# A gated SiLU over 201 MB: loads and stores change queues, most activations and multiplies take 4 rows instead of 2

## Chip, cores, metric

One core of a Trainium2 chip runs the whole program, which uses no other core. The metric is device time in microseconds (us). Before the change: median 471.02 us of 3 runs (470.53 to 471.09).

## The reference

```python
x = randn(32, 512, 2048)              # float32
x1, x2 = x[..., :1024], x[..., 1024:]
out = (x1 * (1 / (1 + exp(-x1)))) * x2   # silu(x1) * x2, float32
```

That is 134.22 MB to read and 67.11 MB to write, with one activation and one multiply per output element.

## The kernel before

The 16,384 rows are cut into 16 tiles of 128 partitions x 8 rows. A tile is one load of 8.39 MB and one store of 4.19 MB; each partition's share is one contiguous piece of 64 KB (load) or 32 KB (store). Two input and two output buffers. ScalarE (ACT) computes silu, VectorE (DVE) multiplies, 2 rows at a time. ScalarE also issues the loads, SyncE (SP) the stores. The first load is placed ahead of the barrier at the program's start.

```python
K, KC = 8, 2
in_pool  = tile_pool(bufs=2);  out_pool = tile_pool(bufs=2)

def load(i):
    xt = in_pool.tile([P, K, in_cols], dt, name="xt")
    nc.scalar.dma_start(out=xt[...], in_=view(x_flat, i))

load(0); load(1)
for i in range(n_tiles):
    ot = out_pool.tile([P, K, half], dt, name="ot")
    for c in range(0, k, KC):
        nc.scalar.activation(out=ot[:, c:ce, :], in_=xt[:, c:ce, :half], func=Silu)
        nc.vector.tensor_mul(out=ot[:, c:ce, :], in0=ot[:, c:ce, :], in1=xt[:, c:ce, half:])
        if last:
            nc.sync.dma_start(out=ov[:, c:ce, :], in_=ot[:, c:ce, :])   # last tile: 4 stores
    if not last:
        nc.sync.dma_start(out=ov, in_=ot[:, :k, :])
    if i + 2 < n_tiles:
        load(i + 2)
# (cut: views, pools' set-up, launch)
```

Of the kernel before, what the change touches and what calls it, by code (L numbers as in the profile page):

```python
# [1 line left out]

# [4 lines left out]


def issue_ahead_of_the_first_barrier(nc):




    head, body = nc.main_func.blocks[:2]
    load = next(ins for ins in body.instructions if type(ins).__name__ == "InstDMACopy")
    at = next(
        j for j, ins in enumerate(head.instructions)
        if ins.engine == load.engine and type(ins).__name__ == "InstDrain"
    )
    body.instructions = [ins for ins in body.instructions if ins.name != load.name]  # L20
    head.instructions = head.instructions[:at] + [load] + head.instructions[at:]


@with_exitstack
def kernel(
    ctx: ExitStack,
    tc: tile.TileContext,
    x: bass.AP,
    out: bass.AP,
):  # L30






    nc = tc.nc
    P = nc.NUM_PARTITIONS

    x_flat = x.flatten_outer_dims()  # L40
    out_flat = out.flatten_outer_dims()
    num_rows, in_cols = x_flat.shape
    half = in_cols // 2
    dt = x_flat.dtype

    K = 8
    KC = 2
    PLAN = [K] * (num_rows // (P * K))

    in_pool = ctx.enter_context(tc.tile_pool(name="in_pool", bufs=2))  # L50
    out_pool = ctx.enter_context(tc.tile_pool(name="out_pool", bufs=2))

    plan = []
    row = 0
    for k in PLAN:
        plan.append((row, k))
        row += P * k
    assert row == num_rows
    n_tiles = len(plan)

    def view(flat, i):
        row0, k = plan[i]
        return flat[row0:row0 + P * k].rearrange("(p k) d -> p k d", k=k)

    nc.at_finalize(issue_ahead_of_the_first_barrier)


    ctx.enter_context(tc.manual_schedule())

    loaded = {}  # L70

    def load(i):
        xt = in_pool.tile([P, K, in_cols], dt, name="xt")
        nc.scalar.dma_start(out=xt[:, :plan[i][1], :], in_=view(x_flat, i))
        loaded[i] = xt

    load(0)
    load(1)
    for i in range(n_tiles):
        k = plan[i][1]  # L80
        xt = loaded.pop(i)
        last = i == n_tiles - 1
        ov = view(out_flat, i)
        ot = out_pool.tile([P, K, half], dt, name="ot")
        for c in range(0, k, KC):
            ce = min(c + KC, k)
            nc.scalar.activation(  # L87
                out=ot[:, c:ce, :],
                in_=xt[:, c:ce, :half],
                func=mybir.ActivationFunctionType.Silu,  # L90
            )
            nc.vector.tensor_mul(  # L92
                out=ot[:, c:ce, :],
                in0=ot[:, c:ce, :],
                in1=xt[:, c:ce, half:],
            )
            if last:
                nc.sync.dma_start(out=ov[:, c:ce, :], in_=ot[:, c:ce, :])
        if not last:
            nc.sync.dma_start(out=ov, in_=ot[:, :k, :])  # L100
        if i + 2 < n_tiles:
            load(i + 2)


# [1 line left out]
_INS = ['x']  # L106
_OUTS = [((32, 512, 1024), 'float32')]


# [23 lines left out]
```

## Time and profile before

| What | Value | Where it is read |
|---|---|---|
| Time | 471.02 us | median of 3 runs |
| Span of the profiled execution | 468.9 us | page, first line |
| VectorE, ScalarE busy | 30%, 25% | page, part 1 |
| DMA engines busy | 99.6% (66.4 + 33.2) | page, part 3 |
| Rate in the middle of the run | 434 GB/s | table of windows |
| First store issued | 32.74 us | timeline |

The page of the kernel before, parts 1 to 3: busy time of the compute engines, busy share of the 16 DMA engines in 40 equal slices (in tenths), and the two DMA queues.

```profile
span 468.9 us, 269 instructions
DVE 142.3 (30%) x64; ACT 118.2 (25%) x65; POOL 0.2 (0%) x4
...
DMA  9899999999999998999999999999999989999998
...
q10 hardware_dynamic: 2304, 134.22, 66.4%
q1 hardware_dynamic: 2736, 67.11, 33.2%
```

The DMA row reads 9 in all slices but four, which read 8 (a digit is the share in tenths, and 9 means 90% or more); no compute engine comes near that. Queue 10 is ScalarE's (loads), queue 1 SyncE's (stores).

The table of windows of the kernel before; the last two columns are the DMA engines' share and GB/s.

```profile
core 0: us, DVE busy (x) ACT busy (x) POOL busy (x), PEclk, DMA share, GB/s
22.00:45.00 23.00, 8.90 (x4) 7.64 (x5) 0.00 (x0) 1.00 0.95 393
45.00:74.00 29.00, 8.89 (x4) 7.32 (x5) 0.00 (x0) 1.00 1.00 434
161.00:277.00 116.00, 35.58 (x16) 29.17 (x17) 0.00 (x0) 1.00 1.00 434
277.00:393.00 116.00, 35.58 (x16) 28.89 (x16) 0.00 (x0) 1.00 1.00 434
```

Every 29 us tile moves 12.58 MB at 434 GB/s. The Trainium skill ("DMA: Bandwidth & Descriptors", section "Where 436 GB/s comes from") works out 435.2 GB/s as the ceiling of the 16 ports; this trace agrees within 0.3%. Only the two ends are below it: the first 45 us, and the last 18 us (375 GB/s from 451 us on).

The timeline of the kernel before: start, duration, engine, instruction.

```profile
21.88 7.31 ACT L87 ACTIVATE ot<-xt 128x2048 f32<-128x2048 f32 x4 [19.31 <-DMA xt<-in_x_dram]
23.82 8.90 DVE L92 TENSOR_TENSOR ot<-ot,xt 128x2048 f32<-128x2048 f32 x4 [23.82 <-ACT ot L87]
...
32.74 23.00 SPq L100 DMA_DIRECT2D out_dram<-ot  x2
32.75 0.35 ACTq L74 DMA_DIRECT2D xt<-in_x_dram  x1
44.54 7.31 ACT L87 ACTIVATE ot<-xt 128x2048 f32<-128x2048 f32 x4 [15.36 <-DMA xt<-in_x_dram]
...
451.03 7.31 ACT L87 ACTIVATE ot<-xt 128x2048 f32<-128x2048 f32 x4 [21.57 <-DMA xt<-in_x_dram]
```

A tile is computed in 10.85 us (21.88 to 32.73); then the store and the load of the tile after next are issued. Load 0 is in SBUF at 21.88, the last one at 451.03 us.

The chain of waits of the kernel before, by engine:

```profile
DMA 80%; DVE 15%; ACT 3%; DVEq 0%; issue 0%
```

The 15% and 3% are not time that faster compute would win: while the chain sits there, the DMA engines move the other load and a store at full rate.

### The profile page before, as it was taken

The numbers are of one execution on the slowest core, as the hardware profiler recorded it, in microseconds if no ns is written. First come the engines' busy times: TensorE is split into PE (matmuls) and PEld (weight loads), VectorE is DVE, ScalarE is ACT, GpSimd is POOL, SyncE is SP. The second block draws the span as 40 slices with busy tenths as digits, with TensorE's granted clock in tenths as the row PEclk, the third lists the DMA queues.
The fourth block names the chain that finished last, engine by engine and source line by source line (L and its number), as shares of the span: only waits on it lengthen the run. The fifth ranks groups of instructions, "written<-read, shape, count | busy, mean of one in ns | idle before, by whom it ended". The sixth has DMA issues, their size and how long they took to land.

```text
span 468.9 us, 269 instructions
## 1 busy us (share of the span) xinstructions
DVE 142.3 (30%) x64; ACT 118.2 (25%) x65; POOL 0.2 (0%) x4
## 2 busy tenths in 40 slices
DVE  0070705106061160601507025070250702407034
ACT  1142406023060330603206032060420604106051
POOL 0000000000000000000000000000000000000000
DMA  9899999999999998999999999999999989999998
GB/s 431 375 447 403 447 447 447 403 419 431 447 447 403 447 492 363 442 492 391 458 403 439 456 447 403 409 442 447 447 403 444 467 386 447 442 419 481 400 409 354
DMA packets 5042, 201.35 MB, mean 429 GB/s; under 512 B 560, under 2 KB 560, under 8 KB 560
## 3 DMA queue, kind: packets, MB, share of 16 engines
q10 hardware_dynamic: 2304, 134.22, 66.4%
q1 hardware_dynamic: 2736, 67.11, 33.2%
q14 instruction: 2, 0.02, 0.0%
HBM read 134.22 MB, written 67.11 MB: 429 GB/s over the span
## 4 chain that ended last, share of the span: by engine, by line
DMA 80%; DVE 15%; ACT 3%; DVEq 0%; issue 0%
DMA xt<-in_x_dram 80%; DVE ot L92 15%; ACT ot L87 3%; DVEq L128 0%
## 5 line engine op out<-in xcount | busy, mean ns | idle before, releaser
L92 DVE TENSOR_TENSOR ot<-ot,xt 128x2048 f32<-128x2048 f32 x64 | 142.3, 2286 | 319.5 <-ACT ot L87 319.5
L87 ACT ACTIVATE ot<-xt 128x2048 f32<-128x2048 f32 x64 | 116.9, 1897 | 338.8 <-DMA xt<-in_x_dram 338.8
L87 ACT ACT_TABLE_LOAD x1 | 1.3, 1283 | 1.3 <-PEq L117 1.3
L117 POOL MEMSET const-uint8-127<- 128x1 uint8 x1 | 0.1, 102 | 0.0
L117 POOL MEMSET const-bfloat16-1.0<- 128x1 bf16 x1 | 0.1, 101 | 0.0
L117 POOL MEMSET const-float32-0.0<- 128x1 f32 x1 | 0.1, 98 | 0.2 <-issue 0.2
L117 POOL MEMSET const-float32-1.0<- 128x1 f32 x1 | 0.1, 98 | 0.0
## 6 DMA issues: line engine op xcount, KB each, us to landing
out_dram<-ot SPq DMA_DIRECT2D x15, 4096.0 KB, 39.8
out_dram<-ot SPq DMA_DIRECT2D x4, 1024.0 KB, 5.7
xt<-in_x_dram ACTq DMA_DIRECT2D x16, 47.1
```

Source lines behind the costliest of these rows:

```text
L87: nc.scalar.activation(out=ot[:, c:ce, :], in_=xt[:, c:ce, :half], func=mybir.ActivationFunctionType.Silu,)
L92: nc.vector.tensor_mul(out=ot[:, c:ce, :], in0=ot[:, c:ce, :], in1=xt[:, c:ce, half:],)
L117: nc = _bacc.Bacc("TRN2", target_bir_lowering=False, num_devices=1)
```

## The change

Its intent: take all waiting for buffers off ScalarE's queue, by giving SyncE the loads (the first still ahead of the barrier) and ScalarE the stores in program order; and pay fewer fixed costs with 4 rows per instruction in all tiles but the last. In the last tile each of the four stores is issued two steps late, so that ScalarE does not wait for VectorE between activations.

```diff
-    KC = 2
+    KC = 4
+    KC_LAST = 2
...
-        nc.scalar.dma_start(out=xt[:, :plan[i][1], :], in_=view(x_flat, i))
+        nc.sync.dma_start(out=xt[:, :plan[i][1], :], in_=view(x_flat, i))
...
+        if i < n_tiles - 1:
+            for c in range(0, K, KC):
+                silu(ot, xt, c, c + KC)
+                mul(ot, xt, c, c + KC)
+            nc.scalar.dma_start(out=ov, in_=ot)
+            if i + 2 < n_tiles:
+                load(i + 2)
+            continue
+
+        cuts = list(range(0, K, KC_LAST))
+        for n, c in enumerate(cuts + [None, None]):
+            if c is not None:
+                silu(ot, xt, c, c + KC_LAST)
+                mul(ot, xt, c, c + KC_LAST)
+            if n >= 2:
+                b = cuts[n - 2]
+                nc.scalar.dma_start(out=ov[:, b:b + KC_LAST, :], in_=ot[:, b:b + KC_LAST, :])
```

(`silu` and `mul` are the two calls of the kernel before, put into functions.)

More of the change, by code (lines that the diff above doesn't have):

```diff
@@ L73, in load, with silu, mul @@
         xt = in_pool.tile([P, K, in_cols], dt, name="xt")
-        nc.scalar.dma_start(out=xt[:, :plan[i][1], :], in_=view(x_flat, i))
+        nc.sync.dma_start(out=xt[:, :plan[i][1], :], in_=view(x_flat, i))
         loaded[i] = xt
+    def silu(ot, xt, c, ce):
+        nc.scalar.activation(
+            out=ot[:, c:ce, :],
+            in_=xt[:, c:ce, :half],
+            func=mybir.ActivationFunctionType.Silu,
+        )
+    def mul(ot, xt, c, ce):
+        nc.vector.tensor_mul(
+            out=ot[:, c:ce, :],
+            in0=ot[:, c:ce, :],
+            in1=xt[:, c:ce, half:],
+        )
     load(0)
@@ L79 @@
     for i in range(n_tiles):
-        k = plan[i][1]
         xt = loaded.pop(i)
-        last = i == n_tiles - 1
         ov = view(out_flat, i)
         ot = out_pool.tile([P, K, half], dt, name="ot")
-        for c in range(0, k, KC):
-            ce = min(c + KC, k)
-            nc.scalar.activation(
-                out=ot[:, c:ce, :],
-                in_=xt[:, c:ce, :half],
-                func=mybir.ActivationFunctionType.Silu,
-            )
-            nc.vector.tensor_mul(
-                out=ot[:, c:ce, :],
-                in0=ot[:, c:ce, :],
-                in1=xt[:, c:ce, half:],
-            )
-            if last:
-                nc.sync.dma_start(out=ov[:, c:ce, :], in_=ot[:, c:ce, :])
-        if not last:
-            nc.sync.dma_start(out=ov, in_=ot[:, :k, :])
-        if i + 2 < n_tiles:
-            load(i + 2)
+        if i < n_tiles - 1:
[14 more added lines that the diff above has]
+                nc.scalar.dma_start(out=ov[:, b:b + KC_LAST, :], in_=ot[:, b:b + KC_LAST, :])
 _INS = ['x']
```

## The prediction

> **What bounds the kernel now.** The DMA engines. The page's slices show them 98-99% busy throughout; VectorE 30%, ScalarE 25%. The table of windows gives 434 GB/s in every steady stretch (44 to 160 us). Successive tiles' activations start 29.0 us apart (timeline); a tile is 8.39 MB read + 4.19 MB written: 434 GB/s. The Trainium skill ("DMA: Bandwidth & Descriptors", "Where 436 GB/s comes from") puts the ceiling of the 16 ports at 435.2 GB/s; the trace agrees within 0.3%. The trace's packet records: a 64 KB load packet takes 2.418 us, a 32 KB store packet 1.213, an 8 KB one 0.309. One engine's share is 128, 120 and 32 of these, an estimated 465.0 us of work; packets run from 1.14 to 467.62 us of the 468.9 us span. So only about 1.5 us of that window is idle. The chain of waits (DMA 80%, DVE 15%, ACT 3%) misleads: while it sits on VectorE, the DMA engines move the other load and a store.
>
> **What the change moves.**
> - Queues swapped: loads to SP, stores to ACT. Same bytes, same transfers. The same page ("Issuing engines are not separate DMA queues") says both feed the same 16 engines; I expect the same packet times. SP's first instruction is 0.13 us ahead of ACT's first issue (trace), so the first load may start about 0.1 us earlier.
> - Activations and multiplies of 4 rows: 1.893 and 2.284 us for 2 rows now; fixed part estimated at 0.15-0.2 us, so 3.6 and 4.4 us for 4. About 5 us saved on each engine, off the critical path, worth nothing. From load landed to store and next load issued: 10.85 us now (timeline), about 12.5 after.
> - Are those 1.6 us hidden? Yes: when a store is issued, the previous one still has about 8 us of packets to go (packet records), and the load in flight about 18 us. Neither queue runs dry. An activation's wait for the store two tiles earlier has about 6 us of slack.
> - ScalarE waits for each tile's last multiply before issuing its store; it idles 22 us per tile for the load anyway.
> - The last tile keeps 2 rows, but its first store now follows the third activation: 5.7 us instead of 4.26 after landing. Its packets are wanted when tile 14's store ends, 8 us after the last load's packets; loads should end about 0.5 us earlier. At most a few tenths of DMA idle. The fourth store is issued at 10.9 us as before, 2.6 us before its turn.
>
> **Critical path.** Practically none of it: -0.1 us at the start, 0 in the middle, 0 to +0.5 us at the end. At most 1.5 us of idle could be won.
>
> **Prediction.** 471.0 us, 8 in 10 between 469.6 and 472.4. Faster by over 2%: 1%; within 2%: 97%; slower by over 2%: 2%.
>
> **What would show it right.** Steady windows at 434 GB/s, tile period 29.0 us; activation about 3.6 us x30, multiply about 4.4 us x30; load landed to next load issue about 12.5 us; the last load landing 0 to 1 us before 451.0; first packet near 1.0 us; span 468.5 to 469.5; the four last stores still back to back.
>
> **What would make it wrong.** Different arbitration or packet times when loads sit on the other queue; a DMA hole (share well under 1.00) in each tile, because the store queue runs dry and loads alone do not reach 434 GB/s; a hole above 1 us before the last tile's first store; the first load not starting early on SP.

## The result

471.81 us, median of 4 runs (471.35, 471.60, 472.01, 472.40), against 471.00 of the kernel before (4 runs by then): ratio 1.002, 95% interval 1.0002 to 1.0037. A ratio is the mean time of one kernel's runs over that of the other's of the same rounds, so it is not quite the ratio of the medians. It is 0.8 us more, and the four runs spread over 1.05 us where the kernel before's spread over 0.56.

The page of the changed kernel, parts 1 to 3:

```profile
span 469.8 us, 207 instructions
DVE 140.3 (30%) x34; ACT 115.4 (25%) x35; POOL 0.2 (0%) x4
...
DMA  9999989999999999999999999999999999999997
...
q1 hardware_dynamic: 2304, 134.22, 66.3%
q10 hardware_dynamic: 2736, 67.11, 33.1%
```

The queues have swapped, bytes and packets are the same, compute is 2 to 3 us less busy, the DMA row is as full. The span is 0.9 us longer.

Its groups of instructions (line, engine, operation, shapes, count, then busy us and mean ns of one):

```profile
L86 DVE TENSOR_TENSOR ot<-ot,xt 128x4096 f32<-128x4096 f32 x30 | 131.4, 4422 | 303.9 <-ACT ot L79 303.9
L79 ACT ACTIVATE ot<-xt 128x4096 f32<-128x4096 f32 x30 | 106.8, 3608 | 321.1 <-DMA xt<-in_x_dram 321.1
```

Its table of windows:

```profile
22.00:45.00 23.00, 8.76 (x2) 6.97 (x2) 0.00 (x0) 1.00 0.99 407
45.00:74.00 29.00, 8.76 (x2) 7.12 (x2) 0.00 (x0) 1.00 1.00 434
161.00:277.00 116.00, 35.04 (x8) 28.49 (x8) 0.00 (x0) 1.00 1.00 434
277.00:393.00 116.00, 35.04 (x8) 28.49 (x8) 0.00 (x0) 1.00 1.00 434
```

The middle is untouched: 434 GB/s, share 1.00. So nothing is lost per tile. Its timeline:

```profile
21.85 7.12 ACT L79 ACTIVATE ot<-xt 128x4096 f32<-128x4096 f32 x2 [19.79 <-DMA xt<-in_x_dram]
25.50 8.76 DVE L86 TENSOR_TENSOR ot<-ot,xt 128x4096 f32<-128x4096 f32 x2 [25.50 <-ACT ot L79]
34.29 0.38 ACTq L102 DMA_DIRECT2D out_dram<-ot  x1
45.85 7.12 ACT L79 ACTIVATE ot<-xt 128x4096 f32<-128x4096 f32 x2 [16.88 <-DMA xt<-in_x_dram]
...
451.92 5.51 ACT L79 ACTIVATE ot<-xt 128x2048 f32<-128x2048 f32 x3 [21.89 <-DMA xt<-in_x_dram]
```

Load 0 lands as before (21.85 against 21.88 us), but load 1 lands at 45.85 instead of 44.54, and the last load at 451.92 instead of 451.03. The loss happens once, between 22 and 46 us, where the first store is issued (34.29 instead of 32.74 us).

The GB/s column does not explain it, because it is a mean over 16 engines, and counts a packet whole in the stretch in which it starts. The packet records do. They carry no engine number, but an engine works through its packets one after another, so that each packet can be chained to the one that ended a few ns before it; that gives 16 chains. L is a 64 KB load packet, S a 32 KB store packet, with start and, in brackets, duration, in us of the span. A steady L lasts 2.42, a steady S 1.21. A load's share on an engine ends with a completion packet of 4 bytes (0.009 us, left out here), which takes a turn of its own between two S. Two typical engines of the kernel before, then a typical one of the changed kernel and its odd one:

```
before, engine a   L33.26(2.44) L35.70(3.18) S38.88(1.21) L40.09(2.42) S42.50(1.21)
before, engine b   L33.45(2.44) L35.89(3.38) S39.26(1.21) L40.47(2.42) S42.89(1.21)
after,  typical    L33.11(2.44) L35.54(2.42) L37.95(3.50) S41.45(1.21) S42.66(1.21) L43.87(2.42)
after,  odd one    L33.49(2.42) L35.90(3.05) S38.94(1.21) L40.15(4.11) S44.26(1.21) S45.47(1.21)
```

Each engine stalls once: the load packet just ahead of its first store takes 0.8 to 1.0 us too long before, 1.0 to 1.6 after. In the changed kernel one engine takes its first store a packet earlier than the other 15, and it pays twice: 0.63 us in the packet before its first store, and 1.69 us in the packet that it works on while the others stall. It ends its share of load 1, completion packet included, at 45.5 us, 2.3 to 2.9 us after the others (42.6 to 43.2). A load has landed only when its slowest engine is done, so load 1 lands late; and the engine stays behind for the rest of the run, because every engine has a fixed share of the transfers (128 L, 120 S and 32 packets of 8 KB each) and none idles to catch up in. Its last packet ends at 468.55 us. The other engines' last packets end between 467.05 and 467.72. In the kernel before all 16 end between 466.8 and 467.63.

The engines are never idle meanwhile: between 22 and 46 us the count of packets in flight never falls below 16 in either kernel.

### The profile page after: what moved, and what is told of

It reads as the page before. It is cut to its first block, busy times and chain, and to the rows that moved or that the text cites. A ratio compares the mean times of both kernels' runs of the same rounds, so it can differ in the third digit from the quotient of the medians.

```text
span 469.8 us, 207 instructions
## 1 busy us (share of the span) xinstructions
DVE 140.3 (30%) x34; ACT 115.4 (25%) x35; POOL 0.2 (0%) x4
## 4 chain that ended last, share of the span: by engine, by line
DMA 77%; DVE 14%; ACT 6%; DVEq 0%; issue 0%; ACTq 0%
DMA xt<-in_x_dram 77%; DVE ot L86 14%; ACT ot L79 6%; DVEq L140 0%; ACTq L79 0%
## 5 line engine op out<-in xcount | busy, mean ns | idle before, releaser
L86 DVE TENSOR_TENSOR ot<-ot,xt 128x4096 f32<-128x4096 f32 (+1 forms) x34 | 140.3, 4170 | 322.5 <-ACT ot L79 322.5
L79 ACT ACTIVATE ot<-xt 128x4096 f32<-128x4096 f32 (+1 forms) x34 | 114.1, 3407 | 343.0 <-DMA xt<-in_x_dram 343.0
## 6 DMA issues: line engine op xcount, KB each, us to landing
xt<-in_x_dram SPq DMA_DIRECT2D x16, 45.5
```

## The experiments

Theory A: the 0.8 us are the effect of one instant. The later first store (34.3 instead of 32.7 us) can catch the 16 engines on different sides of a packet boundary; an engine split off from the rest then ends late. Rivals: Q, the queue swap costs it; T, the late first store of the last tile; R, the longer pipeline of every tile; L, the later the first store, the longer; N, noise between runs.

Each run was timed in 5 rounds beside the kernel before on the same chip, unless a number of runs says otherwise. All results were correct.

### The changed kernel again

> The changed kernel again, for a tighter interval. Its first trace shows one DMA engine whose last packet ends 0.83 us after the next-latest one, and that lost 1.69 us in one load packet when the first store reached the engines. If that straggler is what the 0.8 us are (theory A), this run is again 0.1 to 0.3% above the kernel before and its trace has a last packet about 1 us after most engines' last. If the 0.8 us were noise between runs (rival N), the ratio is within 0.1% of 1.

No edit. Measured: 471.61 us (470.95 to 472.11), ratio 1.0009 (0.9997 to 1.0021). Scattered as before. The profiled execution was one of the quicker ones, 471.04 us, and in it no engine was split off: all first stores start between 41.50 and 42.41 us, and the last packet ends at 468.01. The expectation that every trace would show the straggler was wrong; it comes in some executions. And without a straggler the last load lands at 450.14 us (450.03 in the third trace below), 0.9 to 1.0 us before the 451.03 of the kernel before, as the prediction said.

### 2 rows everywhere, new queues kept

```diff
-    KC = 4
+    KC = 2
```

> Changed kernel with 2 rows in all tiles: only the queue swap and the tail order are left, and the first store is issued at about 32.7 us again instead of 34.3. Theory A (the later first store, through its phase against the 2.42 us load packets, leaves one DMA engine behind): ratio to the kernel before 1.000 within 0.1%, load 1 lands near 44.5 us, no straggler. Rival Q (the queue swap costs it): ratio about 1.002. Rival T (the later first store of the last tile costs it): ratio about 1.002, with load 1 landing near 44.5 us.

Measured: 471.04 us (470.89 to 471.49), ratio 1.0002. First store issued at 32.69, all first stores start at 38.8 to 39.3, no split. So neither the queue swap nor the tail order costs anything that can be seen: Q and T fall. (This execution had a late engine too, its last packet at 468.47; its trace shows two packets near 310 us that were 0.3 and 0.6 us too long. Such a hiccup is another source of the same kind of lateness.)

### 4 rows, old queues and old tail

```diff
+        step = KC if last else 2 * KC
-        for c in range(0, k, KC):
-            ce = min(c + KC, k)
+        for c in range(0, k, step):
+            ce = min(c + step, k)
```

> Kernel before with 4 rows in all tiles but the last, queues and tail as before: first store at about 34.3 us. Theory A: ratio about 1.002, load 1 landing near 45.8 us, a straggling engine at the end. Rivals Q and T: ratio 1.000.

Measured: 471.82 us (470.80 to 472.89, 6 runs), ratio 1.0017 (1.0004 to 1.003). The loss is there with the old queues. Its trace (472.64 us) has one engine with its first store at 39.07 while the others start up to 42.2, a second load packet 1.61 us too long at 40.28, and a last packet that ends at 469.56. As theory A wants it. (About 0.9 us of that end are hiccups of other kinds in later packets of the late engine, at 386, 415 and 457 us.)

### All DMAs on one queue

```diff
-            nc.scalar.dma_start(out=ov, in_=ot)
+            nc.sync.dma_start(out=ov, in_=ot)
```

(and the same for the last tile's stores)

> Changed kernel with all DMAs on SP's queue[...]. In both kernels' traces every engine loses about 0.9 to 1.2 us in the load packet during which the first store of the second queue arrives, and never again. If that loss and the straggler come from a second queue starting beside the first (theory A2), both vanish here: packets at the first store 2.42 us, all engines end within 0.7 us, time about 470.0 us, ratio 0.998. If it comes from the first write to HBM whatever the queue (rival W), the loss stays and the ratio is 0.999 to 1.002.

Measured: 476.25 us (475.84 to 477.02, 4 runs), ratio 1.0115 (1.0101 to 1.013). Theory A2 falls: the stall ahead of the first store is there with one queue too, 1.3 us in the mean, so it does not come from a second queue. And the kernel is clearly slower, though by the 2% rule still "the same". From its page:

```profile
span 472.8 us, 206 instructions
...
DMA  9999999999999999999999999999999999999996
...
q1 hardware_dynamic: 5040, 201.33, 99.1%
```

The engines drift apart: 91 packets were over 60 ns too long, against 33 in the kernel before; eleven engines finish at 467.6 to 467.9 us, five between 468.8 and 471.6. That is 3.9 us of span. Another 1.2 us lie outside the span (time less span is 2.5 to 3.1 us in its runs, 1.7 to 1.8 in all others). Why one queue does either stays open.

### 4 rows in tile 0 alone

```diff
-            for c in range(0, K, KC):
-                silu(ot, xt, c, c + KC)
-                mul(ot, xt, c, c + KC)
+            parts = [0, 4, 8] if i == 0 else [0, 2, 4, 6, 8]
+            for c, ce in zip(parts, parts[1:]):
+                silu(ot, xt, c, ce)
+                mul(ot, xt, c, ce)
```

> Changed kernel with 4 rows in tile 0 alone, 2 rows in all other tiles: the first store is issued at about 34.3 us, all later tiles have the shorter pipeline. Theory A (the instant of the very first store decides, once): ratio about 1.001 to 1.002 in the mean, runs scattered up to 472.5 us, in traces with a straggler one load packet near 38 to 44 us is 1.6 us too long. Rival R (the longer pipeline of every tile costs it): ratio 1.000 like the kernel with 2 rows everywhere (1.0002).

Measured: 471.54 us (471.31 to 472.36), ratio 1.0013 (0.9999 to 1.0026), mean 0.76 us above the kernel before. The profiled execution (472.36 us) has the split: one first store at 38.92, the others up to 41.95, a load packet 1.65 us too long at 40.13, the last packet at 469.33. Changing tile 0 alone brings the split, and in the mean the loss, with an interval that just reaches 1; this speaks against R. (Of the late end, 0.84 us is a hiccup near 311 us, which by the chains fell on the late engine.) It also shows how one late engine hurts the rest: the last load lands late, the last tile's first store is issued at 457.05 us (455.47 in the last version below, which has the same tail and no split), and for 0.2 to 0.9 us all other engines have nothing to do between 457.1 and 458.1 us, the hole that the prediction had feared for another reason.

### Tile 0 in 5 and 3 rows

Edit as above, with `[0, 5, 8] if i == 0 else [0, 4, 8]`.

> Changed kernel, tile 0 cut into 5 and 3 rows: first store at about 35.2 us, later than in the changed kernel, so that it reaches the engines in the middle of a 2.42 us load packet (near 39.0 us) and not at the boundary between two (38.0 to 38.4 us). Theory A: no engine is split off from the others at the first store, the mean ratio is back at 1.000 to 1.001. Rival L (the later the first store, the longer): ratio 1.002 or more.

Measured: 471.16 us (470.88 to 471.38), ratio 1.0005 (0.9992 to 1.0017), mean 0.21 us above. First store issued at 35.10, later than in the changed kernel; no split (41.68 to 42.16). My arithmetic for where the arrival falls between packets was too simple: the stall sits in the same packet as in the changed kernel. What holds is that no engine was split off and the time is lower. L is in doubt.

### Tile 0 in 3 and 5 rows

Edit as above, with `[0, 3, 8] if i == 0 else [0, 4, 8]`.

> Changed kernel, tile 0 cut into 3 and 5 rows: first store at about 33.5 us, reaching the engines near 37.3 us, mid-packet. Theory A: no split, ratio 1.000 to 1.001. Rival L: about halfway between 2 rows (1.0002) and 4 rows (1.001 to 1.002), so 1.001. Rival R: 1.001 to 1.002.

Measured: 471.09 us (470.98 to 472.25), ratio 1.0009 (0.9996 to 1.0021). The first store was issued at 34.59, not at 33.5: I had overlooked that the first multiply ends early and the second waits for the 5-row activation. So this run is no test of an earlier arrival, but a fourth version with the first store near 34.5 us. Four runs lie at 471.0 to 471.2 and one at 472.25; the profiled one (471.01) has no split.

### A small store early

```diff
     load(0)
+    # (cut: the pool and the scratch tensor)
+    wt = warm_pool.tile([P, 128], dt, name="wt")
+    nc.vector.memset(wt, 0.0)
+    nc.scalar.dma_start(out=scratch, in_=wt)     # 64 KB to a scratch tensor
     load(1)
```

(with 2 rows everywhere)

> Changed kernel with 2 rows everywhere, plus a 64 KB store of zeros to a scratch tensor on ACT's queue while load 0 runs. Theory W (the first write, whatever the queue, stalls every engine once by about 0.9 us): the stall moves to the scratch store near 2 to 5 us and is gone near 36 us; as the engines are busy there too, time stays within 0.1% of the kernel before, unless it overlaps the 0.7 us that the first load packets lose anyway, then ratio about 0.999. Rival (the stall belongs to the first large store or to its 128 descriptors of 32 KB): packets near 36 us stay 0.9 us too long and the ratio is 1.000 to 1.001.

Measured: 471.34 us (471.24 to 471.62), ratio 1.0011 (0.9998 to 1.0023). The stall near 36 us is still there, 0.83 us in the mean. So it is not the first write as such, of any size. What sets the first large store apart stays open. The small store won nothing: its runs lie 0.5 us above the kernel before in the mean, with no engine split off, so a split is not the only source of such a loss.

### The changed kernel a third time, and its first store delayed by one packet and by half a packet

```diff
+        if i == 0:
+            nc.scalar.activation(out=ot[:, 4:8, :692], in_=xt[:, 4:8, :692], func=Silu)
```

This extra activation of tile 0 (its result is overwritten by the real one) delays the first store by 2.4 us; with `6:8` and `:660` by 1.2 us.

> Changed kernel once more beside the next two. First store at 34.3 to 34.5 us. Mean 0.6 to 0.8 us above the kernel before, runs scattered from 471.0 to 472.5.

> Changed kernel with one extra activation in tile 0 that delays its first store by about 2.4 us, one load packet, to about 36.75 us. Theory A (the first store splits the engines when it reaches them at a boundary between load packets): the arrival is again at a boundary, so mean and scatter are like the changed kernel's, 0.5 us or more above the kernel before, and a split in the trace is likely. Rival L (later is slower): clearly slower than the changed kernel, 1 us or more. Rival (only the earlier kernels' other differences mattered): like the kernel before.

> The same with a delay of about 1.2 us, half a load packet: first store at about 35.5 us, arrival in mid-packet. Theory A: no split in the trace, all runs within 0.5 us of the kernel before's median, mean about 0.3 us above it as with 5 and 3 rows. Rival L: between the changed kernel and the kernel with one packet's delay.

Measured, on another chip than the runs above: changed kernel 471.18 us (470.94 to 471.86), ratio 1.0000; one packet later (issued at 36.76) 471.02 us (470.94 to 471.15), ratio 0.9995; half a packet later (35.40) 471.13 us (470.75 to 471.67), ratio 0.9998. No single engine was split off in the three profiled executions. But with one packet's delay the engines fell into two groups: nine start their first store at 41.76 to 42.35 us, and seven move one more load packet first and start it at 43.99 to 44.40. Each of the 16 has its one long packet, the one that starts near 38 us; none has a second one over 0.14 us too long near there, and the last packet ends at 468.03. So a split as such does not cost: what the lone engine pays for is the second long packet (1.6 to 1.7 us), spent while the others have their one. Two of my expectations missed: the changed kernel was not 0.6 us slower here, and a delay of a whole packet, though it brought a split, brought no loss, so the simple rule "at a packet boundary" is not the right one. L finds no support: the version with the latest first store of all is the steadiest, and not slower. But as the changed kernel itself lost nothing on this chip, these two runs could hardly show a loss, and test no more than that.

### 2 rows in tile 0, 4 rows in tiles 1 to 14

Edit as above, with `[0, 2, 4, 6, 8] if i == 0 else [0, 4, 8]`.

> The changed kernel with 2 rows in tile 0 (first store near 32.7 us) and 4 rows in tiles 1 to 14. Theory A in the form the traces leave (what counts is whether one engine takes its first store a packet before the others, which happened only with the first store issued between 34.25 and 34.5 us): all engines start their first store within 38.8 to 39.4 us, no straggler from it, mean within 0.2 us of the kernel before, all runs below 471.8 us. Rival R (4 rows in every tile cost it): 0.5 us or more above the kernel before, runs up to 472.5 us.

Measured, on a third chip: 470.85 us (470.56 to 471.08), ratio 0.9999 (0.9985 to 1.0013). First store issued at 32.77; all first stores between 38.83 and 39.46; last packet at 467.50. Its table of windows:

```profile
22.00:45.00 23.00, 8.90 (x4) 7.43 (x5) 0.00 (x0) 1.00 0.96 399
45.00:74.00 29.00, 8.76 (x2) 7.07 (x3) 0.00 (x0) 1.00 1.00 434
```

This is the changed kernel but for tile 0, and no loss is seen. The changed kernel did not run on this chip, and on the second chip it lost nothing either, so this run alone does not clear the longer pipeline; with the two runs that had 4 rows in tiles 1 to 14 on the first chip (5 and 3 rows 0.21 us above the kernel before, 3 and 5 rows 0.41, both means), and 4 rows in tile 0 alone 0.76 above, R is unlikely. It is the version to keep if one wants the change's fewer instructions; it does not beat the kernel before.

### The traces side by side

"First stores" is when the first and the last of the 16 engines start their first store packet; "last packet" is the end of the last packet of all; "time" is that of the profiled execution, "difference" the time less the last packet.

| Version | First store issued | First stores | Engine split off | Last packet | Time | Difference |
|---|---|---|---|---|---|---|
| before | 32.74 | 38.88 to 39.26 | no | 467.63 | 470.65 | 3.02 |
| 2 rows everywhere | 32.69 | 38.82 to 39.33 | no | 468.47 | 471.49 | 3.02 |
| 2 rows in tile 0 | 32.77 | 38.83 to 39.46 | no | 467.50 | 470.57 | 3.07 |
| 2 rows, early small store | 33.22 | 38.93 to 39.87 | no | 468.23 | 471.34 | 3.11 |
| changed, 1st trace | 34.29 | 38.94 to 41.94 | yes | 468.55 | 471.60 | 3.05 |
| changed, 2nd trace | 34.42 | 41.50 to 42.41 | no | 468.01 | 471.04 | 3.03 |
| changed, 3rd trace | 34.25 | 41.69 to 42.37 | no | 468.19 | 471.27 | 3.08 |
| 4 rows in tile 0 alone | 34.35 | 38.92 to 41.95 | yes | 469.33 | 472.36 | 3.03 |
| 4 rows, old queues | 34.47 | 39.07 to 42.23 | yes | 469.56 | 472.64 | 3.08 |
| 3 and 5 rows | 34.59 | 41.48 to 42.23 | no | 467.94 | 471.01 | 3.07 |
| 5 and 3 rows | 35.10 | 41.68 to 42.16 | no | 468.08 | 471.16 | 3.08 |
| half a packet later | 35.40 | 41.46 to 42.07 | no | 467.92 | 470.98 | 3.06 |
| one packet later | 36.76 | 41.76 to 44.40 | nine to seven | 468.03 | 471.11 | 3.08 |

Three things stand in it. With two queues the time is the end of the last DMA packet plus 3.02 to 3.11 us, in all 13 executions. The three executions with one engine split off are the three slowest; less the hiccups named above, their last packets end at an estimated 468.5 to 468.6 us (469.33 - 0.84, 469.56 - 0.93, and 468.55). And this split of one engine came only with a first store issued between 34.25 and 34.6 us, where the first store packets change from 38.9 to 41.5 us: versions issued earlier start them all at 38.8 to 39.9, versions issued later all at 41.5 or after. Issuing in between is a coin toss; three of these six traces have it.

The untraced runs agree. Of the 30 runs of versions with the first store at 34.25 to 34.6 us (changed kernel 14, the other three 16), 15 took over 471.5 us and the mean is 471.57. Of the 30 runs of the other six versions with two queues, 2 did, and the mean is 471.11. Of 42 runs of the kernel before, 5 did (three of them in the rounds on the other chip), and the mean is 471.01. These sets come from several chips. On the chip of the first eight experiments alone it is 11 of 21, against 1 of 15 and, for the kernel before, 2 of 20: noise (N) does not explain that. On the chip of the two delays it is 1 of 5, against 1 of 10 and 3 of 9: there the changed kernel shows no loss at all. Why chips should differ stays open. Six of the 30 runs were traced: the three over 471.5 us have an engine split off, the three below have not. For the other 12 late runs a split is not shown.

## Why the prediction was right

It said 471.0 us, 469.6 to 472.4, and "within 2%"; 471.81 was measured. The reason it gave is the one that holds: the DMA engines bound both kernels, and what the change moves lies beside them. The small loss on top came from a step that it did not have. Point by point:

- *DMA bounds the kernel; steady windows at 434 GB/s.* Right: 434 GB/s and share 1.00 in both, and a tile period of 29.0 us (activations at 74.92 and 103.92 us). The "98-99%" of its first lines is a misreading of the slices' digits 9 and 8; part 3 of the page gives 99.6%.
- *The queue swap is worth nothing.* Right; 2 rows with the new queues and new tail gave 1.0002.
- *The first load starts about 0.1 us earlier.* Right: the first packet starts at 0.99 us instead of 1.14.
- *Activation about 3.6 us, multiply about 4.4 us; about 12.5 us from landing to store.* Right: 3.608, 4.422, and 34.29 - 21.85 = 12.44. "About 5 us saved on each engine" was too much: ScalarE 2.8 (118.2 - 115.4), VectorE 2.0 us. I had not considered that successive instructions already overlap: four activations of 1.893 us take 7.31 us, 0.26 less than their sum, and four multiplies of 2.284 us take 8.90, 0.24 less; two longer ones take 7.12 and 8.76. Two instructions of 2 rows, each by itself, are 0.19 (ScalarE) and 0.15 us (VectorE) longer than one of 4 rows; about half of that was hidden already. It is off the critical path either way.
- *The longer pipeline is hidden; "0 in the middle".* Right for every tile in which it repeats: 4 rows in tiles 1 to 14 gave 0.9999, and in the changed kernel the store before still has 7.4 us of packets to go when the next is issued (7.2 to 7.9 before the change; packet records). What failed is the silent step that a delay hidden in the steady state is hidden in tile 0 too. There the delay moves the first store from a moment at which all engines take it up together to one at which sometimes one of them takes it up a packet before the rest, pays for two long packets, and ends 0.8 to 1.8 us after the next-latest (hiccups included). In the other two traces of the changed kernel this did not happen.
- *"Only about 1.5 us of that window is idle."* Wrongly named. The engines are not idle; the 1.5 us are packets that take too long, about 0.6 us in each engine's first load packet and 0.9 ahead of its first store. Such time is not to be won by keeping queues full.
- *The last load lands 0 to 1 us before 451.0.* Wrong in the first trace, 451.92; right in the second and third, 450.14 and 450.03. The reasoning (loads get ahead when the store comes later) held for 15 engines: their share of load 1 ends at 42.6 to 43.2 us instead of 43.7 to 44.1. The odd engine's ends at 45.5, and a landing is the slowest engine's.
- *0 to +0.5 us at the end.* The sign was right by luck, the place was not: the surplus is made near 38 us and shows at the end. The span, 469.8 us, lay above the stated 468.5 to 469.5.

Left open: what the stall ahead of the first store is; what decides which engine takes the store up early; why one engine that goes ahead alone pays twice and nine of 16 do not; why the loss did not show on the second chip; what one queue loses.

## What to carry to other kernels

When the DMA engines are busy from end to end at the port rate, swapping the two queues and merging instructions moves next to nothing (here 0 to 0.8 us of 471; one queue for everything did cost 1.15%); say so and look elsewhere. What is left is the difference between the 16 engines: in these traces each has a fixed share of the transfers, a load lands with its slowest engine (45.47 us for the last completion packet, 45.85 for the activation), and an engine that fell behind once stayed behind to the end, so look at the end of the last packet of each engine and not at the mean rate. A loss that appears in some of the executions is judged by many runs, and by changing the one tile where the trace first differs.

## What the Trainium skill lacked or had wrong

- "DMA: Bandwidth & Descriptors", "Rules for kernel authors", says of spreading DMAs over issuing engines for bandwidth that it "Doesn't help". Here the changed kernel took 476.25 us with all its DMAs on one queue, against 471.61 on two (medians on the same chip): 1.0% in favour of two queues. Its span was 472.8 us against 469.3 in the traced executions, with five engines late. One version of one kernel, and the cause is open.
- The same page, "Where 436 GB/s comes from", says that the HBM side (about 358 GB/s) binds for transfers between HBM and SBUF. This one-core program moved 434 GB/s of mixed reads and writes over 400 us, at the 435.2 GB/s of the ports. ("HBM Reference", "Specifications (TRN2)", does say that a core alone measures above its share, and gives about 425.)
- The same page, "Queues, rings and completion order", describes round-robin by packet between queues; the trace agrees, with 64 KB load packets of 2.42 us and 32 KB store packets of 1.21 us in turn. It does not say that one load packet of every engine takes about 0.8 to 1.6 us longer (0.6 on the engine that goes ahead alone) at about the time of the first large store, on one queue or two, and that this is not seen at later stores.
- No page says that an engine which falls behind once does not catch up: here by 0.8 to 1.8 us (hiccups included), to the end of the run, with the time 3.02 to 3.11 us after the last packet.
